# A router that works by halves of a row, behind the output projection of a two-layer decoder

## The chip, the cores and the metric

The kernel runs on one core of one Trainium2 chip. The metric is the device time of one execution in microseconds (us). Before the change the median of three runs is 1393.88 us (1393.7 to 1397.09).

## The reference

528 tokens (512 and 16 prepended meta tokens) of width 1024 pass two layers, float32 throughout. Layer 0 mixes tokens with a short gated convolution, layer 1 with attention over a shared latent. Behind each mixer stands a mixture of experts, and this is the part that matters here:

```
h = h + (mixer output) @ w_out              # 1024 x 1024
xf = rmsnorm(h, g)
g_logits = xf @ w_grp                       # 8 groups
e_logits = (xf @ w_exp).reshape(n, 8, 8)    # 8 experts in each group
grp   = argmax(g_logits)                    # one group per token
e_in  = e_logits[grp];  top 2 of 8 experts in it
gate  = max(softmax(g_logits)) * top_p / sum(top_p)
y     = sum over the two experts of gate * (silu(x @ w_gate) * (x @ w_up)) @ w_down
h = h + y
```

There are 64 experts in each layer with three matrices of 1024 x 256 floats, 1 MB each. All of them are read in each layer. At the end a last RMSNorm is taken and the 512 tokens are written.

## The kernel before

The residual stream `h` lies in SBUF as four tiles of 128 tokens and, in layer 0, a fifth tile of the 16 meta tokens (`META`). A tile is 128 tokens by 1024.

**Weights.** All large weights pass through one ring of 8 KB-per-partition slots (`Ring`, L67). They are loaded in the order of use by the queue of SyncE (SP, line L101). A load is issued when a slot comes free, and the router's weights are a load of their own (L347): in layer 0 on the same queue, in layer 1 on ScalarE's. GpSimdE multiplies them by the norm's gain (L348).

**Output projection** (`project_out`, L256). It is done for two halves of 512 output columns. In a half each tile has a PSUM bank (tag `acc`, five banks), and the contraction is walked in steps of one or two blocks of 128 rows; a block is three fp32r matmuls per tile (high and low parts of both operands, L292). Before a step its weight rows are split into high and low parts by ScalarE (L211) and VectorE (L212). The meta tile uses plain fp32 matmuls in four quarters of a bank (L274); ScalarE copies them into the scratch tile `x0[0]`, and a matmul with `fold` adds the quarters into a bank with the tag `misc` (L286). When the last step of a tile is done, VectorE adds the bank to `h` (L294). After the second half of a tile, `done(t)` calls the router for it.

**Router** (`Moe.route`, L363, one tile). ScalarE squares the row with a sum (L231), with `x0[0]` as its waste output, and GpSimdE makes the scale of the norm (L232, L233). TensorE transposes the row in two sets of four 128 x 128 blocks (L372) through one bank with the tag `tp`; the first set is copied out by ScalarE into `hT` (one buffer, L375), the second by VectorE into `x0[1]` (L377). Eight fp32 matmuls (each is two records in the trace) make 72 logits in the bank `misc` (L380), which has one buffer. VectorE then works out group and experts (L383 to L403), and two small copies are ScalarE's (L388, L396); the result is a mask `M`. `rank` (L409) counts, with small bf16 matmuls into a bank `rk`, which place each token has in its group (L417, L422, L425), and VectorE makes a selection matrix `d` (L418 to L421).

**First gather and experts.** `first_gather` (L457) collects the first group's tokens with matmuls of `d` and `h` (L431), scales them, and selects the tokens of the first four experts (L450). Then `run` starts: `gate_up` (L585, L589) multiplies with the gate and up weights of four experts and releases their slots, `down` (L628, L621) with the down weights. 16 such steps of four experts make a layer.

**Order.** Outside of `run`, where TensorE's order is that of the text, a planner orders the instructions of each engine: it simulates them with a cost model and takes, of what is ready, what stands first in the text. On the chip each engine then works off its list in order.

The function that is called for each finished tile is given here:

```
project_out(..., zH, zL, zM, STEPS[0], lambda t: moe0.route(t, psum))      # layer 0, L976
project_out(..., *oT[1], None, STEPS[1], lambda t: moe1.route(t, psum))    # layer 1, L1342
```

Of the kernel before, what the change touches and what calls it, by code (L numbers as in the profile page):

```python
# [9 lines left out]
F32 = mybir.dt.float32  # L10
F32R = mybir.dt.float32r
BF16 = mybir.dt.bfloat16
I32 = mybir.dt.int32
AF = mybir.ActivationFunctionType
ALU = mybir.AluOpType
# [4 lines left out]
P = 128  # L20
D = 1024
# [3 lines left out]
META = 4  # L25
NE = 64
CAP = 32
EPS = 1e-6
# [8 lines left out]
STEPS = ((0,), (1,), (2,), (3,), (4,), (5,), (6, 7)), ((4,), (5,), (6, 7))  # L37
# [79 lines left out]
def trunk_kernel(ctx: ExitStack, tc: tile.TileContext, x, meta, const, masks, rope, gcol, grow, wr, w_in, w_out, w_a, w_qr, w_hp,  # L117
# [17 lines left out]
    for l in range(2):  # L135
        for a in range(4):
            c = G_FFN + 8 * l + 2 * a
# [97 lines left out]
    def chunk(t, k):  # L235
        return h[t][:rows(t)].rearrange("r (a p b) -> r a b p", a=4, b=2)[:, k // 2, k % 2]
# [19 lines left out]
    def project_out(weights, psum, name, zH, zL, zM, steps, done):  # L256


        tiles = ((META,) if zM is not None else ()) + (0, 1, 2, 3)
        off = 0 if zM is not None else NM  # L260
        base = 0 if zM is not None else 4
        first, last = steps[0][0], steps[-1][-1]
        for half in range(2):
            ps = {t: psum.tile([P, 512], F32, tag="acc", name="acc", bufs=5) for t in tiles}
            for step in steps:
                w = {}
                for j in step:
                    kg, v = j // 4, j % 4
                    raw = ring.get((name, half, kg))[:, v]
                    w[j] = weights(j)  # L270
                    split(*w[j], raw)
                    if v == 3:
                        for i in range(4 if zM is not None else 0):
                            T.matmul(ps[META][32 * i:32 * i + 32], zM[:, j - 3 + i], ring.get((name, half, kg))[:, i],  # L274
                                     start=j - 3 == first, stop=j == last)
                        ring.release((name, half, kg))
                for t in tiles:
                    n = rows(t)
                    hh = h[t][:n, 512 * half:512 * half + 512]
                    pt = ps[t]  # L280
                    if t == META:
                        if last in step:
                            sm = moe0.x0[0].rearrange("p a s -> p (a s)")
                            A.activation(sm, pt, AF.Copy)
                            pt = psum.tile([P, 512], F32, tag="misc", name="misc", bufs=1)
                            T.matmul(pt[:n], fold, sm, start=True, stop=True)  # L286
                    else:
                        c = col0(t) - off
                        for j in step:
                            wH, wL = w[j]  # L290
                            for m, (l, r) in enumerate(((zH, wH), (zH, wL), (zL, wH))):
                                T.matmul(pt, l[:, j - base, c:c + n], r, start=j == first and m == 0, stop=j == last and m == 2)  # L292
                    if last in step:
                        V.tensor_tensor(hh, hh, pt[:n], op=ALU.add)  # L294
                        if half == 1:
                            done(t)


    class Moe:
# [35 lines left out]
        def prepare(self, limit):  # L335

            nT = self.nT
            n = NR[self.layer]
            m = n - TOP[self.layer]
            if self.layer == 1:  # L340
                self.first_tiles("right")
            R = self.R = [(pool(self.right if i < m else self.top, f"ringR{self.layer}{i}", side="right"), f"R{i}") for i in range(n)]
            for i in RIGHT[self.layer]:
                ring.open([R[i]], limit if i >= m else None)
            rp = self.rp = pool(self.temp, f"rt{self.layer}", 2, side="right")
            self.wg = rp.tile([P, 8, 72], F32, name="wg", bufs=1)
            (nc.scalar if self.layer else nc.sync).dma_start(self.wg, wr[self.layer].rearrange("p (a c) -> p a c", a=8))  # L347
            G.tensor_tensor(self.wg, self.wg, self.g[:, :, None].to_broadcast([P, 8, 72]), op=ALU.mult)  # L348
            self.rks = ExitStack()
            self.rkp = pool(self.rks, f"rk{self.layer}", side="right", space=PSUM)  # L350
            self.M = rp.tile([P, nT, 72], BF16, name="M", bufs=1)
            self.gl = rp.tile([P, nT, 8], F32, name="gl", bufs=1)
            self.gm = rp.tile([P, nT, 1], F32, name="gm", bufs=1)
            self.s8 = rp.tile([P, nT, 8], F32, name="s8", bufs=1)
            self.r8 = rp.tile([P, nT, 8], F32, name="r8", bufs=1)
            self.done = []
            G.tensor_copy(self.aux[:, :, 8], tok1[:, :nT])
            if nT == 5:
                for a in (self.gl, self.gm, self.oh, self.s8, self.r8, self.M):
                    G.memset(a[:, META], 0.0)  # L360
                G.memset(self.rstd[:, META:], 1.0)

        def route(self, t, psum):  # L363

            rp, n = self.rp, rows(t)
            rs = self.rstd[:n, t:t + 1]
            rstd_of(rp, rs, h[t][:n], n, D, junk=self.x0[0].rearrange("p k s -> p (k s)").bitcast(BF16))
            hT = []
            for u in range(2):
                ps = psum.tile([P, 4, P], F32, tag="tp", name="tp", bufs=1)  # L370
                for k in range(4):
                    T.transpose(ps[:, k, :n], chunk(t, 4 * u + k), ident[:n, :n])  # L372
                hT.append(rp.tile([P, 4, P], F32, tag="hT", name="hT", bufs=1) if u == 0 else self.x0[1])
                if u == 0:
                    A.activation(hT[u][:, :, :n], ps[:, :, :n], AF.Copy)  # L375
                else:
                    V.tensor_copy(hT[u][:, :, :n], ps[:, :, :n])  # L377
            ps = psum.tile([P, 512], F32, tag="misc", name="misc", bufs=1)
            for k in range(8):
                T.matmul(ps[:n, :72], hT[k // 4][:, k % 4, :n], self.wg[:, k], start=k == 0, stop=k == 7)  # L380

            gl, gm, oh = self.gl[:n, t], self.gm[:n, t], self.oh[:n, t]
            V.reduce_max(gm, ps[:n, :8], axis=AX)  # L383
            V.scalar_tensor_tensor(oh, ps[:n, :8], gm, rev8[:n], op0=ALU.is_equal, op1=ALU.mult)
            mg = rp.tile([P, 1], F32, tag="mg", name="mg")[:n]
            V.reduce_max(mg, oh, axis=AX)
            V.tensor_scalar(oh, oh, mg, None, op0=ALU.is_equal)
            A.activation(self.M[:n, t, NE:], oh, AF.Copy)  # L388

            se = rp.tile([P, 8, 8], F32, tag="se", name="se", bufs=1)[:n]  # L390
            gt = rp.tile([P, 8, 8], F32, tag="gt", name="gt", bufs=1)[:n]
            eq = rp.tile([P, 8, 8], F32, tag="eq", name="eq", bufs=1)[:n]
            s8, r8, M = self.s8[:n, t], self.r8[:n, t], self.M
            sh = [n, 8, 8]
            V.tensor_tensor(se, ps[:n, 8:72].rearrange("p (g e) -> p g e", g=8), oh[:, :, None].to_broadcast(sh), op=ALU.mult)
            A.activation(gl, ps[:n, :8], AF.Copy)  # L396
            V.reduce_sum(s8, se.rearrange("p g e -> p e g"), axis=AX)
            V.tensor_tensor(eq, s8[:, None, :].to_broadcast(sh), s8[:, :, None].to_broadcast(sh), op=ALU.is_equal)
            V.tensor_tensor(gt, s8[:, None, :].to_broadcast(sh), s8[:, :, None].to_broadcast(sh), op=ALU.is_gt)
            V.tensor_tensor(eq, eq, before8[:n], op=ALU.mult)  # L400
            V.tensor_tensor(gt, gt, eq, op=ALU.add)
            V.reduce_sum(r8, gt, axis=AX)
            V.scalar_tensor_tensor(M[:n, t, :NE].rearrange("p (g e) -> p g e", g=8), r8[:, None, :].to_broadcast(sh), 2.0,  # L403
                                   oh[:, :, None].to_broadcast(sh), op0=ALU.is_lt, op1=ALU.mult)
            self.done.append(t)
            if len(self.done) < self.nT:
                self.rank(t)
# [474 lines left out]
    with ExitStack() as l0:  # L882
# [10 lines left out]
        with ExitStack() as l0a:  # L893
# [44 lines left out]
            for j in range(4):  # L938
                W = []
                for s in range(3):  # L940
# [33 lines left out]
        wp = pool(l0, "wp0b", 2)  # L974
        psum = pool(l0, "ps0b", space=PSUM)
        project_out(lambda j: [wp.tile([P, 512], F32R, tag=a, name=a) for a in ("wH", "wL")], psum, "out", zH, zL, zM, STEPS[0],  # L976
                    lambda t: moe0.route(t, psum))
        moe0.first_gather(psum)


# [358 lines left out]
            whole[:] = weights(SLOT)  # L1339
        return [w[:, 512 * (j - 4):512 * (j - 3)] for w in whole]  # L1340

    project_out(part, psum, "o", *oT[1], None, STEPS[1], lambda t: moe1.route(t, psum))  # L1342
    moe1.first_gather(psum)
    psum_stack.close()
    oproj.close()
# [129 lines left out]
```

## Time and profile before

| | before |
|---|---|
| median of three runs | 1393.88 us |
| the profiled execution | 1390.24 us |
| its span, first to last instruction | 1388.4 us |
| TensorE busy (weight loads apart) | 1243.8 us, 90% |
| VectorE, ScalarE, GpSimdE busy | 507.5, 313.5, 53.6 us |
| HBM read and written | 434.40 and 2.10 MB, 314 GB/s over the span |
| TensorE clock granted, mean | 0.96 |

The table is of one execution, taken by the hardware profiler. Engines have short names in the views: PE is TensorE's matmuls and PEld its weight loads, DVE is VectorE, ACT ScalarE, POOL GpSimdE, SP SyncE; a q behind a name is that engine's issue of DMAs. L292 is line 292 of the kernel before. Times are us from the span's start. The ends of matmuls are modelled, so that a stretch in which PE is busy throughout is not by that alone one at its peak; the distance of the starts tells more. In a row of instructions, what stands in brackets is the idle time of the engine before it and what ended it.

### The profile page before, as it was taken

To read this page: it belongs to the slowest core of one execution; us is meant where nothing else is said; L and a number is where in the kernel's file an instruction comes from. 1 tells how busy PE (TensorE), PEld (TensorE's weight loads), DVE (VectorE), ACT (ScalarE), POOL (GpSimd) and SP (SyncE) were. 2 spreads that over 40 slices of the span, in tenths; PEclk is the share of its full clock that TensorE was granted. 3 is DMA by queue.
4 is the path that set the end of the run, shared out by engine and by line. 5 is a ranking of instruction groups with operands and counts; after the bars stand their busy time and mean duration, and the time that the engine had idled before them with its cause. 6 is when DMAs were issued, how large, how long until landed. Compare 5 with 4: busy or idle time off the path is not lost.

```text
span 1388.4 us, 22912 instructions
## 1 busy us (share of the span) xinstructions
PE 1243.8 (90%) x9647; PEld 794.1 (57%) x9647; DVE 507.5 (37%) x1220; ACT 313.5 (23%) x712; POOL 53.6 (4%) x146
## 2 busy tenths in 40 slices
PE   7999999999888888879799999999988788888885
PEld 7999866544444344434388888864543334433432
DVE  5555336132231312234246776462230212213024
ACT  6333123011010010121154765231110010101013
POOL 2100101000000000000021000010000000000001
PEclk9999999999999999989999999999999998999998
DMA  7422563899999999999910022949999999999994
GB/s 285 154 91 90 208 253 154 351 420 420 419 419 420 419 421 418 420 420 421 366 41 28 32 92 101 369 179 418 419 420 419 421 418 421 420 419 420 420 418 173
DMA packets 65954, 438.09 MB, mean 316 GB/s; under 512 B 7457, under 2 KB 7841, under 8 KB 15282
## 3 DMA queue, kind: packets, MB, share of 16 engines
q1 hardware_dynamic: 64432, 434.74, 76.8%
q10 hardware_dynamic: 1154, 1.78, 0.4%
q8 instruction: 78, 1.28, 0.4%
q14 instruction: 34, 0.28, 0.1%
q0 software_dynamic: 256, 0.01, 0.0%
HBM read 434.40 MB, written 2.10 MB: 314 GB/s over the span
## 4 chain that ended last, share of the span: by engine, by line
DMA 26%; PE 21%; ACT 1%; DVE 1%; issue 1%; POOL 0%; POOLq 0%; ACTq 0%; SPq 0%; DVEq 0%
DMA R<-in_w_gate_dram 6%; DMA B<-in_w_down_dram 4%; DMA B<-in_w_up_dram 4%; DMA R<-in_w_up_dram 3%; DMA A<-in_w_up_dram 3%; PE gu L589 2%; PE a L1062 2%; PE sc L1225 2%; PE pj L1319 2%; PE acc L292 2%; DMA A<-in_w_gate_dram 1%; DMA A<-in_w_down_dram 1%; DMA B<-in_w_gate_dram 1%; DMA R<-in_w_down_dram 1%; PE pj L1205 1%; PE ot L1274 1%
## 5 line engine op out<-in xcount | busy, mean ns | idle before, releaser
L589 PE MATMUL gu<-R,xT 128*32 128x256 f32 x1856 | 161.7, 409 | 34.3 <-DMA R<-in_w_up_dram 19.4
L589 PE MATMUL gu<-B,xT 128*32 128x256 f32 x1376 | 148.3, 438 | 38.7 <-DMA B<-in_w_gate_dram 22.1
L589 PEld LDWEIGHTS gu<-R,xT 128*32 128x32 f32 x1856 | 77.7, 117 | 107.6 <-issue 30.3
L589 PEld LDWEIGHTS gu<-B,xT 128*32 128x32 f32 x1376 | 66.9, 125 | 99.6 <-DMA B<-in_w_gate_dram 30.6
L589 PE MATMUL gu<-A,xT 128*32 128x256 f32 x720 | 101.3, 421 | 18.6 <-DMA A<-in_w_up_dram 11.8
L431 PE MATMUL w<-h,d 128*128 128x512 f32 x224 | 99.7, 598 | 0.0
L562 DVE COPY ag<-w 128x18 f32<-128x18 f32 x14 | 2.5, 177 | 240.0 <-PE w L561 240.0
L596 ACT ACTIVATE sg<-gu 128x256 f32<-128x256 f32 x32 | 12.3, 385 | 327.9 <-PE gu L589 327.9
L631 ACT ACTIVATE y<-dn 128x512 f32<-128x512 f32 x60 | 35.8, 597 | 198.1 <-PE dn L621 191.0
L950 PE MATMUL acc<-xH,wH 128*128 128x264 f32 x384 | 79.1, 286 | 0.0
L950 PE MATMUL acc<-xL,wH 128*128 128x264 f32 x384 | 78.8, 286 | 0.0
L950 PE MATMUL acc<-xH,wL 128*128 128x264 f32 x384 | 77.6, 283 | 0.0
L589 PEld LDWEIGHTS gu<-A,xT 128*32 128x32 f32 x720 | 45.8, 120 | 51.8 <-DMA A<-in_w_up_dram 15.7
L657 PE MATMUL w<-yHL,d 128*128 128x512 f32 (+1 forms) x252 | 73.0, 422 | 0.3
L659 DVE TENSOR_TENSOR h<-h,w 128x512 f32<-128x512 f32 x112 | 69.6, 679 | 0.8 <-PE w L657 0.5
L450 PE MATMUL w<-sel,xg 128*128 128x128 f32 x480 | 64.8, 292 | 4.5 <-ACT xg L436 4.5
L431 PEld LDWEIGHTS w<-h,d 128*128 128x128 f32 x224 | 41.4, 190 | 47.1 <-issue 46.4
L215 ACT ACTIVATE wH<-A,gc 128x256 fp32r<-128x256 f32 (+1 forms) x119 | 52.8, 520 | 59.0 <-PE acc L950 35.5
L450 PEld LDWEIGHTS w<-sel,xg 128*128 128x128 f32 x480 | 60.7, 205 | 7.2 <-ACT xg L436 7.2
L621 PE MATMUL dn<-R,sg 128*32 128x512 f32 x472 | 63.7, 595 | 0.0
L950 PEld LDWEIGHTS acc<-xL,wH 128*128 128x128 f32 x384 | 59.9, 188 | 0.2 <-DVE xL L212 0.2
L950 PEld LDWEIGHTS acc<-xH,wL 128*128 128x128 f32 x384 | 59.7, 189 | 0.0
(379 smaller groups left out, 2072.1 us busy)
## 6 DMA issues: line engine op xcount, KB each, us to landing
R<-in_w_up_dram SPq DMA_DIRECT2D x58, 1024.0 KB, 19.9
R<-in_w_down_dram SPq DMA_DIRECT2D x58, 1024.0 KB, 19.9
R<-in_w_gate_dram SPq DMA_DIRECT2D x58, 1024.0 KB, 19.9
B<-in_w_gate_dram SPq DMA_DIRECT2D x44, 1024.0 KB, 19.8
B<-in_w_up_dram SPq DMA_DIRECT2D x42, 1024.0 KB, 19.8
B<-in_w_down_dram SPq DMA_DIRECT2D x32, 1024.0 KB, 19.8
A<-in_w_down_dram SPq DMA_DIRECT2D x27, 1024.0 KB, 19.8
A<-in_w_gate_dram SPq DMA_DIRECT2D x26, 1024.0 KB, 19.9
```

Source lines behind the costliest of these rows:

```text
L215: i = A.activation(H, src, AF.Copy, scale=g)
L292: T.matmul(pt, l[:, j - base, c:c + n], r, start=j == first and m == 0, stop=j == last and m == 2)
L431: i = T.matmul(ps[u], d, h[t][:n, 512 * u:512 * u + 512], start=first, stop=last, skip_group_check=True)
L450: T.matmul(ps[:, k], self.xg[:, 4 * u + k], self.sel[q], start=True, stop=True)
L589: T.matmul(gu[CAP * e:CAP * e + CAP, s], xT[k // 4][:, k % 4, CAP * e:CAP * e + CAP], w[e][:, k], start=k == 0, stop=k == 7)
L621: T.matmul(dn[CAP * e:CAP * e + CAP, :n], hT[:, b, CAP * e:CAP * e + CAP], w[:, b, c:c + n], start=b == 0, stop=b == 1)
L631: A.activation(y[:, u], down_part(q, hT, u, 0, 512 * u, 512), AF.Copy)
L657: T.matmul(ps[:m, :n], DT[t], a, start=i == 0, stop=i == 1)
L659: V.tensor_tensor(hh, hh, ps[:m, :n], op=ALU.add)
L950: T.matmul(ps[:, u, :HALF], l[:, k, P * m:P * m + P], r[:, k, HALF * u:HALF * u + HALF], start=k == 0 and l is wH and r is xH, stop=k == 7 ...
L1062: T.matmul(a[:n, b, :c1 - c0], l[:, k, :n], r[:, k, c0:c1], start=k == 0 and m == 0, stop=k == 7 and m == 2)
L1225: T.matmul(ps[u][:, :w], l[:, q], r[:, w * u:w * u + w], start=m == 0, stop=m == 4 and u < nb - 1)
```

## The change

The router gets a second argument, the half `u`, and is called after both halves of a tile. At the first call it takes the squares of the first 512 columns, the first four transposes and the first four logit matmuls; at the second the rest, and then everything as before. The sums of squares lie in a new small tile `sq`, and GpSimdE adds the halves up. The logits of all tiles lie side by side in one bank, which is held from the first call on (`lg`, 72 columns per tile); only the very first matmul in it has the start flag. Tile 0 comes ahead of the meta tile in both halves, and the meta tile's fold uses the transposes' bank.

```diff
     def project_out(weights, psum, name, zH, zL, zM, steps, done):
-        tiles = ((META,) if zM is not None else ()) + (0, 1, 2, 3)
+        tiles = (0,) + ((META,) if zM is not None else ()) + (1, 2, 3)
...
                             A.activation(sm, pt, AF.Copy)
-                            pt = psum.tile([P, 512], F32, tag="misc", name="misc", bufs=1)
+                            pt = psum.tile([P, 512], F32, tag="tp", name="fold", bufs=1)
                             T.matmul(pt[:n], fold, sm, start=True, stop=True)
...
                     if last in step:
                         V.tensor_tensor(hh, hh, pt[:n], op=ALU.add)
-                        if half == 1:
-                            done(t)
+                        done(t, half)
...
             self.r8 = rp.tile([P, nT, 8], F32, name="r8", bufs=1)
+            self.sq = rp.tile([P, nT, 2], F32, name="sq", bufs=1)
+            self.lg = None
...
-        def route(self, t, psum):
+        def route(self, t, u, psum):
 
             rp, n = self.rp, rows(t)
-            rs = self.rstd[:n, t:t + 1]
-            rstd_of(rp, rs, h[t][:n], n, D, junk=self.x0[0].rearrange("p k s -> p (k s)").bitcast(BF16))
-            hT = []
-            for u in range(2):
-                ps = psum.tile([P, 4, P], F32, tag="tp", name="tp", bufs=1)
-                for k in range(4):
-                    T.transpose(ps[:, k, :n], chunk(t, 4 * u + k), ident[:n, :n])
-                hT.append(rp.tile([P, 4, P], F32, tag="hT", name="hT", bufs=1) if u == 0 else self.x0[1])
-                if u == 0:
-                    A.activation(hT[u][:, :, :n], ps[:, :, :n], AF.Copy)
-                else:
-                    V.tensor_copy(hT[u][:, :, :n], ps[:, :, :n])
-            ps = psum.tile([P, 512], F32, tag="misc", name="misc", bufs=1)
-            for k in range(8):
-                T.matmul(ps[:n, :72], hT[k // 4][:, k % 4, :n], self.wg[:, k], start=k == 0, stop=k == 7)
+            rs, c = self.rstd[:n, t:t + 1], slice(512 * u, 512 * u + 512)
+            junk = self.x0[0].rearrange("p k s -> p (k s)").bitcast(BF16)
+            A.activation(junk[:n, :512], h[t][:n, c], AF.Square, accum_out=self.sq[:n, t, u:u + 1])
+            G.tensor_scalar(self.sq[:n, t, u:u + 1], self.sq[:n, t, u:u + 1], 1.0 / D, EPS if u == 0 else self.sq[:n, t, 0:1],
+                            op0=ALU.mult, op1=ALU.add)
+            ps = psum.tile([P, 4, P], F32, tag="tp", name="tp", bufs=1)
+            for k in range(4):
+                T.transpose(ps[:, k, :n], chunk(t, 4 * u + k), ident[:n, :n])
+            if u == 0:
+                hT = rp.tile([P, 4, P], F32, tag="hT", name="hT", bufs=1)
+                A.activation(hT[:, :, :n], ps[:, :, :n], AF.Copy)
+            else:
+                hT = self.x0[1]
+                V.tensor_copy(hT[:, :, :n], ps[:, :, :n])
+            if self.lg is None:
+                self.lg = psum.tile([P, 512], F32, tag="misc", name="misc", bufs=1)
+                assert n == P
+            ps = self.lg[:, 72 * t:72 * t + 72]
+            for k in range(4):
+                T.matmul(ps[:n], hT[:, k, :n], self.wg[:, 4 * u + k], start=u == 0 and t == 0 and k == 0, stop=u == 1 and k == 3,
+                         skip_group_check=True)
+            if u == 0:
+                return
+            G.tensor_tensor(rs, self.sq[:n, t, 1:2], nhalf[:n], op=ALU.pow)
...
-                    lambda t: moe0.route(t, psum))
+                    lambda t, u: moe0.route(t, u, psum))
...
-    project_out(part, psum, "o", *oT[1], None, STEPS[1], lambda t: moe1.route(t, psum))
+    project_out(part, psum, "o", *oT[1], None, STEPS[1], lambda t, u: moe1.route(t, u, psum))
```

## Rows read from the trace of the kernel before

**Rows 1.** The page's 40 slices of the span: busy share of DMA in tenths.

```profile
DMA  7422563899999999999910022949999999999994
```

**Rows 2.** Windows over both expert stages: length, engines' busy us (instructions), PEclk, DMA share, GB/s.

```profile
244.00:640.00 396.00, 352.84 (x2960) 176.28 (x2952) 102.54 (x216) 49.02 (x98) 0.00 (x0) 0.95 1.00 415
...
937.00:1385.00 448.00, 375.91 (x3151) 185.71 (x3139) 110.55 (x225) 55.79 (x113) 5.05 (x12) 0.94 0.98 404
```

**Rows 3.** Load queue in time (start, length, engine, line, what), first loads after each silence.

```profile
247.04 0.80 SPq L101 DMA_DIRECT2D R<-in_w_down_dram  x2
...
935.52 0.81 SPq L101 DMA_DIRECT2D A<-in_w_down_dram  x2
```

**Rows 4.** Windows: PE, PEld, DVE, ACT, POOL busy; layer 0's second half and tail, layer 1's.

```profile
186.00:204.00 18.00, 18.00 (x86) 12.86 (x84) 4.26 (x7) 3.90 (x7) 1.15 (x1) 1.00 0.37 146
...
204.00:223.00 19.00, 19.00 (x118) 13.66 (x118) 11.77 (x48) 8.90 (x21) 4.62 (x15) 1.00 0.40 141
223.00:230.00 7.00, 7.00 (x32) 5.78 (x32) 2.52 (x10) 0.00 (x0) 0.00 (x0) 0.52 1.01 425
230.00:244.00 14.00, 12.77 (x75) 7.89 (x77) 10.68 (x55) 4.14 (x10) 0.00 (x0) 1.00 0.12 49
884.70:902.50 17.80, 17.80 (x80) 14.75 (x80) 6.52 (x10) 2.68 (x5) 1.15 (x1) 1.00 0.96 385
902.50:924.60 22.10, 22.05 (x145) 17.60 (x144) 15.79 (x63) 7.87 (x20) 3.73 (x12) 1.00 0.68 264
924.60:931.85 7.25, 4.65 (x24) 2.88 (x25) 5.57 (x33) 2.98 (x5) 0.00 (x0) 1.00 0.08 33
```

**Rows 5.** Timeline of PE in layer 1: transposes and logits between projection matmuls.

```profile
902.56 0.63 PE L372 MATMUL tp<-cs,h 128*128 128x128 f32 x4
902.94 0.47 PE L292 MATMUL acc<-wH,oH 128*128 128x512 f32 x1
903.26 0.40 PE L292 MATMUL acc<-wL,oH 128*128 128x512 f32 x1
...
904.46 1.01 PE L380 MATMUL misc<-wg,hT 128*128 128x72 f32 x8
905.27 0.48 PE L292 MATMUL acc<-wL,oH 128*128 128x512 f32 x1
```

**Rows 6.** Timeline of DVE in layer 1: first add; last tile's chain and rank.

```profile
902.75 0.69 DVE L294 TENSOR_TENSOR h<-h,acc 128x512 f32<-128x512 f32 x1 [6.12 <-PE acc L292]
...
922.38 0.16 DVE L383 TENSOR_REDUCE gm<-misc 128x1 f32<-128x8 f32 x1
...
924.90 0.22 DVE L403 SCALAR_TENSOR_TENSOR M<-r,oh 128x64 bf16<-128x64 f32 x1
925.42 0.23 DVE L418 SCALAR_TENSOR_TENSOR rm<-rk,M 128x72 f32<-128x72 f32 x1 [0.30 <-PE rk L417]
...
925.89 0.26 DVE L421 TENSOR_REDUCE aux<-rm 128x8 f32<-128x64 f32 x1
```

**Rows 7.** Layer 0's router weights and first-half add; the masks' landing time and conversion.

```profile
186.68 1.15 POOL L348 TENSOR_TENSOR wg<-wg,gc 128x576 f32<-128x576 f32 x1 [27.62 <-DMA wg<-in_wr_dram]
...
180.28 0.69 DVE L294 TENSOR_TENSOR h<-h,acc 128x512 f32<-128x512 f32 x1
...
8.03 0.33 SPq L890 DMA_DIRECT2D xT<-in_masks_dram  x1
...
DMA to landing us min/median/max: 12.2/12.2/12.2
...
24.68 0.29 POOL L891 CAST tri_b<-xT 128x128 bf16<-128x128 f32 x1
```

**Rows 8.** Timeline of PE: the meta tile's gather, first gate/up matmuls of both layers.

```profile
221.63 1.12 PE L431 MATMUL acc<-hm,d 16*128 16x512 f32 x2
...
243.37 7.11 PE L589 MATMUL gu<-R,xT 128*32 128x256 f32 x128
...
931.85 0.41 PE L589 MATMUL gu<-A,xT 128*32 128x256 f32 x2 [0.78 <-DVE xT L451]
```

## The prediction

> **What bounds the kernel now.** I read the page's row of DMA load in 40 slices first, then busy time by stretch, then the load queue, then the engines in order of time around both routers. The DMA row [rows 1] stands at 9 in slices 8 to 19 and 27 to 38, counted from 0: both expert stages run at the rate of their weights, 415 and 404 GB/s, while TensorE idles there (352.8 of 396 us in the first) [rows 2]. So an expert stage lasts as long as its loads, and these are held up by one thing: with all slots full the queue is silent until the first gate/up matmuls of that layer release a slot. In layer 0 the DMA share is 0.12 in 230 to 244 [rows 4] and the next load goes out at 247.0; in layer 1 the next goes out at 935.5 [rows 3]. Whatever moves the first gate/up matmul (243.4 and 931.9 [rows 8]) therefore moves the end of the kernel one for one, once per layer. The change works just ahead of these two points.
>
> What bounds that stretch? In the second half of the output projection TensorE is busy 18.00 of 18.00 us (layer 0, 186 to 204) and 17.80 of 17.80 (layer 1, both halves), 80 matmuls at 0.223 us each [rows 4]. And in the router's tail too: 19.00 of 19.00 and 7.00 of 7.00 in layer 0, 22.05 of 22.10 in layer 1. Only at the very end does it idle, 7.25 - 4.65 = 2.6 us in layer 1 and 14.00 - 12.77 = 1.2 in layer 0. Latency chains are there, but gathers and the remaining projection matmuls fill them. In layer 0 one thing more is lost: in 223 to 230 the granted clock is 0.52 [rows 4], mostly at 1.2 GHz. That stretch costs 7.0 x (1 - 0.52) = 3.4 us.
>
> **The change part by part.** *Work moved.* For each tile four transposes and four chunks of logits (eight matmul records) leave the tail and go into the second half's matmuls. Four transposes take 902.94 - 902.56 = 0.38 us and the projection matmul behind them 903.26 - 902.94 = 0.32 instead of 0.22, so 0.10 more; the logits 905.27 - 904.46 = 0.81 [rows 5] and again 0.10. That is 1.39 us per tile, 5.6 us in layer 1, all of it added to a stretch without a gap; in layer 0 the 16-row tile is bounded by 0 and 1.39, I take 0.7, so 6.3 us. The tail loses the same work, 0.38 + 0.81 = 1.19 per tile, and between none and all of the switches, since there they partly stood beside other fp32 work. So TensorE's sum over both stretches does not fall: it rises by 0 to 0.8 us per layer, I take 0.4.
>
> *Layer 1.* TensorE's floor is before, plus 0.4, less the idle that could be filled: of the 2.6 us, all but about 1.0 is the closing chain (gathered tokens, selection, first xT), which is not touched. So -0.6 at best. The other end is VectorE, whose work in the tail stays whole: add 0.69 and a copy of the same 512 columns, the chain from group maximum to mask 922.38 to 925.13 = 2.75, rank 925.42 to 926.15 = 0.73 [rows 6]: 4.86 us per tile, 19.4 for four if nothing overlaps. Before, the tail from the first add (902.75 [rows 6]) to the last rank took 926.15 - 902.75 = 23.4. After, it starts 5.6 later. With 19.4 and about 2 of lead-in for the first tile (transposes, copy, logits) it ends 21.4 - (23.4 - 5.6) = 3.6 later than before. VectorE was in fact busy 15.79 us in 902.5 to 924.6 [rows 4], nearer to 17 for the whole tail than to 19.4, so the lower end is the nearer: +1.2.
>
> The waits in the tail change little. The logits of a tile now go into the shared bank, and must still wait until VectorE and ScalarE have read the previous tile's; with the one-buffered bank of before they did that too. The 16-row tile's fold takes the transposes' bank, which delays the next transposes by its 1.0 us matmul and an add; the tail has over 4 us per tile, so that is covered. The scratch copy for the fold now follows tile 0's square on ScalarE, about 1.5 us, covered by projection matmuls of the other tiles (0 to 0.5 uncovered, I take 0).
>
> *Layer 0.* If the low-clock stretch goes, -3.4 + 0.4 + 0.5 (VectorE, as above but with one more tile as cover) = -2.5. If it stays, +0.4 + 0.5 = +0.9. The 16-row gathers just ahead of it (two records of 1.1 us, at 221.6 [rows 8]) are in the changed kernel as well. I take the middle, -0.8.
>
> *ScalarE, GpSimdE.* Two half squares for one whole one, one more small GpSimdE operation per tile. ScalarE is busy 3.90 of 18 us in the second half, VectorE 4.26 [rows 4], but the splits of the next weight rows run on both, in order, and now can stand behind a square or a copy of about 0.6 us. A row of weights lasts 12 matmuls, 2.7 us, its two splits are 512-column operations of about 0.7 each [rows 6], so some 1 us is in hand: 0 to 1 us in all, I take 0.5. GpSimdE's results are first needed by the gathers, 20 us later: nothing.
>
> *Loads.* The last early loads are released by the last projection matmuls. In layer 0 they have landed by about 232 (share 0.12 from 230 on [rows 4]), 11 us ahead of the first gate/up; a few us later costs nothing, and from 11 us on it costs one for one.
>
> *A new wait.* In layer 0 the first half's logits need the router weights. GpSimdE scales these as soon as they land, at 186.7 to 187.8, after a wait of 27.6 us; tile 0's first-half add is at 180.3 [rows 7], and with tile 0 ahead of the 16-row tile about 179.5. Transposes and copy bring its logits to about 181.5. If they stand there in TensorE's queue, everything behind them, the whole second half, waits: 0 to 6.3 us. If the planner put them behind enough matmuls, nothing. What it thinks of such a load: the masks, issued at 8.0 behind the first weights, landed 12.2 us later, at 20.2, and the planner put their conversion at 24.7, behind operations that were written later but that it took to be ready sooner [rows 7]. It was pessimistic there, so I take 0.
>
> Sum: 1.2 - 0.8 + 0.5 = +0.9, so 1390.24 + 0.9 = 1391.1 us for an execution like the profiled one (span 1388.4 and 1.8 around it). The median of the runs shown is 1393.88, 3.6 above it: 1394.8.
>
> The Trainium skill's page "TensorE: Matmul & The Clock Gate", section "Part 4: PE-mode transpose", says that transposes do not count towards the full clock as matmuls do. Against it stands that layer 1 has as many transposes per tile and stays at 1.00, and that the clock fell after a stretch with TensorE busy all the time [rows 4]. By the rule the drop would go, since half of the transposes leave the tail: the second rival below.
>
> **Rivals.** *One: the tail is latency after all.* Ends of matmuls are modelled, so "busy" may cover waits; then the tail loses its 6.3 and 5.6 us, and the second halves take the work in without growing: -11.9 + 0.9 = -11 us, 1383. For: VectorE's chain is serial per tile. Against: 0.223 us per projection matmul leaves no room, and the tail's pieces start without gaps. 0.12.
>
> *Two: the low-clock stretch goes and the tail packs well.* -2.5 in layer 0, -0.6 in layer 1, 0.5 for the splits: -2.6, 1391.3; at best, with no cost of switches, VectorE or splits, -3.4 - 1.0 = -4.4, 1389.5. For: fewer small operations stand ahead of it. Against: the 16-row gathers stay. 0.12.
>
> *Three, slower: the router weights stop TensorE in layer 0.* It decides from the point where tile 0's first-half logits reach the head of the queue before 187.8; each us earlier costs one. Worst 6.3 + 0.9 = +7.2, 1401.1; from half of it on, +4.1, 1398.0, it can be told. Against: the masks. 0.17.
>
> *Four: the planner leaves the first halves in the tail,* since it orders by readiness and not by the text: 0, 1393.9. In the order of before it did take ready transposes ahead of projection matmuls. 0.05.
>
> **How the numbers follow.** Forecast 0.54; its own range, from the bounds (layer 1 -0.6 to +3.6, layer 0 -2.5 to +0.9, splits 0 to 1: -3.1 to +5.5), is 1391 to 1399. A measurement tells about 0.3%, 4.2 us, from no change. Faster: rival one, 0.05 of rival two at its best, 0.03 of the forecast: 0.20. Slower: rival three 0.17 and 0.07 of the forecast, where VectorE's end holds in both layers: 0.24. Same: the rest, 0.56. The range leaves rival one out and reaches to the end of rival three: 1389 to 1401.
>
> **What would show it.** Right: transposes and logits of all tiles between the projection's second-half matmuls, these as dense as before; that half longer by 5 to 7 us per layer; the tail shorter by about as much; more idle TensorE in the tail; first gate/up within 3 us of before in each layer. Wrong: the first gate/up over 4 us earlier (rivals one and two, told apart by the granted clock around 230), or TensorE waiting on the router weights around 182 to 188 (three). An expert stage that does not shift with its first gate/up would break the one-for-one rule.

## The result and the profile after

The changed kernel takes 1402.17 us (median of six runs, 1400.04 to 1404.54) against 1393.10 for the kernel before (six runs, 1390.76 to 1397.09): a ratio of 1.0057, with an interval of 1.0042 to 1.0072. It is slower by about 8 us, 7.4 us above the 1394.8 that was predicted and 1.2 us above the range, which ended at 1401. The profiled execution has a span of 1398.2 us, 9.8 above the 1388.4 of before.

Where do the 9.8 us arise? The next fence has windows of the kernel after (length; PE, PEld, DVE, ACT, POOL busy; granted clock; DMA share; GB/s). The first runs from the first projection matmul of layer 0 to its first gate/up matmul, the last is the same for layer 1.

```profile
157.81:252.44 94.63, 91.00 (x416) 59.87 (x415) 38.77 (x134) 24.57 (x57) 8.51 (x27) 0.91 0.54 215
186.60:204.00 17.40, 17.40 (x96) 12.69 (x95) 3.59 (x6) 5.34 (x13) 2.25 (x4) 1.00 0.39 145
204.00:223.00 19.00, 19.00 (x101) 13.37 (x100) 8.05 (x24) 6.12 (x15) 3.54 (x11) 1.00 0.21 63
232.00:252.44 20.44, 18.52 (x53) 9.39 (x53) 10.72 (x61) 3.76 (x9) 0.00 (x0) 0.58 0.18 76
894.10:943.66 49.56, 45.89 (x249) 34.75 (x248) 26.71 (x105) 15.27 (x38) 6.07 (x17) 1.00 0.65 261
```

The same two windows of the kernel before:

```profile
157.43:243.37 85.94, 84.07 (x417) 59.14 (x415) 39.64 (x134) 23.23 (x47) 6.67 (x22) 0.96 0.59 236
884.74:931.85 47.11, 44.47 (x248) 35.19 (x248) 27.83 (x105) 13.53 (x30) 4.88 (x13) 1.00 0.69 274
```

Layer 0's stretch grew by 94.63 - 85.94 = 8.69 us, layer 1's by 49.56 - 47.11 = 2.45. The rest is small: the stretch starts 0.38 later; from layer 0's first gate/up to layer 1's projection it is 641.66 us against 641.37; and behind layer 1's first gate/up 2.01 us come back (454.54 against 456.55). The sum is 0.38 + 8.69 + 0.29 + 2.45 - 2.01 = 9.8. Most of what comes back is the last gate/up step, whose matmuls ran at the lower clock before and not after. That is not the work of the change: e12 below, whose layer 1 is that of before, has the short piece too (3.64 us), e5 the long one (5.33). The last such piece in the chain of waits, before and then after:

```profile
1355.81 5.33 PE gu L589 x58
```

```profile
1367.53 3.64 PE gu L599 x58
```

The lines that answer to [rows 8], [rows 7] and [rows 5], from the timeline of the kernel after (start, length, engine, line, operation):

```profile
180.25 0.75 PE L374 MATMUL tp<-cs,h 128*128 128x128 f32 x4
180.75 0.47 PE L292 MATMUL acc<-wL,zH 128*128 128x512 f32 x1
181.06 0.39 PE L292 MATMUL acc<-wH,zL 128*128 128x512 f32 x1
...
189.01 1.15 POOL L347 TENSOR_TENSOR wg<-wg,gc 128x576 f32<-128x576 f32 x1
...
195.82 0.90 PE L386 MATMUL misc<-wg,hT 128*128 128x72 f32 x7
...
229.67 1.10 PE L441 MATMUL acc<-hm,d 16*128 16x512 f32 x2
230.70 1.11 PE L386 MATMUL misc<-wg,xT 128*128 128x72 f32 x8
231.74 1.59 PE L441 MATMUL acc<-hm,d 16*128 16x512 f32 x2
...
234.16 2.07 PE L441 MATMUL acc<-h,d 128*128 128x512 f32 x2
...
252.44 3.88 PE L599 MATMUL gu<-R,xT 128*32 128x256 f32 x68
```

The change does what it says: transposes and logits stand among the second half's matmuls, four transposes taking 0.50 us (180.25 to 180.75) and the matmul behind them 0.31, where the prediction had 0.38 and 0.32. Half 2 stays dense (17.40 of 17.40 us), and VectorE, which in 204 to 223 was busy 11.77 us before [rows 4], is so for 8.05: its chains start later. The router weights are scaled at 189.0, and TensorE first uses them at 195.8, without a wait. What is new comes late. The meta tile's gathers are at 229.7 and 231.7 instead of 220.5 and 221.6, and behind them the next gather takes 2.07 us: from 232 to the first gate/up the granted clock is 0.58, most of it spent at 1.2 GHz. Before, the low stretch took some 7 us at 0.52 [rows 4].

The second new thing is idle TensorE in the tail. Who it waited for, in layer 0 from 205 us to the first gate/up: after, then before (the wait; total us, times, longest).

```profile
PE rk L432 <- DVE rm L428: 1.0, 3, 0.3
PE acc L460 <- ACT xg L446: 0.8, 1, 0.8
PE tp L374 <- DVE xT L380: 0.5, 1, 0.5
PE tp L374 <- DVE rm L428: 0.3, 1, 0.3
PE acc L477 <- DVE oh L397: 0.3, 1, 0.3
```

```profile
PE acc L450 <- ACT xg L436: 0.8, 1, 0.8
PE rk L422 <- DVE rm L418: 0.3, 1, 0.3
```

### The profile page after: what moved, and what is told of

Same layout as the page of the kernel before. It is cut to its first block, busy times and chain, and to the rows that moved or that the text cites. A ratio compares the mean times of both kernels' runs of the same rounds, so it can differ in the third digit from the quotient of the medians.

```text
span 1398.2 us, 22957 instructions
## 1 busy us (share of the span) xinstructions
PE 1250.7 (89%) x9647; PEld 793.6 (57%) x9647; DVE 505.3 (36%) x1220; ACT 316.3 (23%) x730; POOL 56.6 (4%) x155
## 3 DMA queue, kind: packets, MB, share of 16 engines
q8 instruction: 78, 1.28, 0.4%
## 5 line engine op out<-in xcount | busy, mean ns | idle before, releaser
L599 PE MATMUL gu<-R,xT 128*32 128x256 f32 x1856 | 158.9, 399 | 36.6 <-DMA R<-in_w_up_dram 25.6
L599 PE MATMUL gu<-B,xT 128*32 128x256 f32 x1376 | 145.5, 437 | 36.3 <-DMA B<-in_w_gate_dram 18.4
```

The costliest lines, as they stand in the source:

```text
L599: T.matmul(gu[CAP * e:CAP * e + CAP, s], xT[k // 4][:, k % 4, CAP * e:CAP * e + CAP], w[e][:, k], start=k == 0, stop=k == 7)
```

## The experiments

Every experiment is read by the same two windows as above, from the first projection matmul to the first gate/up matmul of the layer, in the one traced execution of each kernel. These are steadier than the whole: layer 1's window is 47.11 to 47.14 us in all seven kernels whose layer 1 is that of before. The stretch between the two windows is not: it takes 641.4 to 648.3 us over the fourteen traces, with the same code in it, and the traces of before and after happen to have the two shortest. The whole kernel's time varies by several us between executions of one kernel, so each time stands beside that of the kernel before from the same chip: 1394.08 us for e1 to e4, 1395.71 for e5 to e8, 1393.65 for e9 to e12.

**e1 and e2: the change in one layer alone.** The other layer keeps the whole route of before.

```
 e1:  project_out(..., lambda t, u: moe1.route_whole(t, psum) if u else None)
 e2:  project_out(..., lambda t, u: moe0.route_whole(t, psum) if u else None)   # and the meta tile first
```

> Halves in layer 0 alone; layer 1 routes whole rows as before. Theory A (the loss is layer 0's longer stretch at 1.2 GHz, plus some switching): first gate/up of layer 0 again about 9 us later than before, low clock for about 16 us; layer 1 as before from there; total +7 to +9 us, about 1401. Theory B (VectorE's chain bounds both tails, the clock is a side issue): each layer carries its share, so about +4 to +5 here, 1397.5.

> Halves in layer 1 alone; layer 0 as before. Theory A: +2.5 us at layer 1's first gate/up, as between the two traces (1.0 of it TensorE idle, 1.4 TensorE work), total about +2 to +3, 1395.5; no low clock in layer 1's tail. Theory B: +4 to +5, 1397.5.

Measured: e1 1400.89 us (1391.62 to 1403.02 over nine runs, two of them near 1392), ratio 1.0025 (1.0004 to 1.0046); e2 1395.32 (1390.87 to 1399.51), ratio 1.0002 (0.9988 to 1.0017). Windows of e1, then of e2:

```profile
158.01:252.60 94.59, 90.97 (x417) 59.89 (x415) 38.75 (x134) 24.56 (x57) 8.49 (x27) 0.91 0.54 215
897.59:944.73 47.14, 44.49 (x248) 35.23 (x248) 27.81 (x105) 13.51 (x30) 4.86 (x13) 1.00 0.69 274
```

```profile
158.41:244.21 85.80, 83.92 (x416) 58.60 (x414) 39.60 (x134) 23.23 (x47) 6.65 (x22) 0.96 0.60 237
890.13:939.71 49.58, 45.92 (x249) 34.78 (x248) 26.71 (x105) 15.27 (x38) 6.04 (x17) 1.00 0.66 261
```

The layers do not touch each other: e1 has layer 0's window of after (94.59) and layer 1's of before (47.14), e2 the reverse. Layer 0 carries the loss. The two runs of e1 near 1392 show a higher mean clock (0.960 and 0.962) than the other seven (0.952 to 0.959), so the long low stretch may have stayed away in them; no trace of them is kept. In the whole time layer 1's 2.5 us can't be told from nothing.

**e3 and e4: the meta gathers over 128 rows,** in the kernel after and the kernel before.

```
+    G.memset(h[META], 0.0)
     nc.sync.dma_start(h[META][:NM], meta)
 ...
-            n, d = rows(t), self.d[:rows(t), t].bitcast(F32)
+            d = self.d[:, t].bitcast(F32)
-                i = T.matmul(ps[u], d, h[t][:n, 512 * u:512 * u + 512], ...)
+                i = T.matmul(ps[u], d, h[t][:, 512 * u:512 * u + 512], ...)
```

> The changed kernel, with the meta tile's gather matmuls over 128 rows in place of 16 (rows 16 to 127 are zero on both sides); same number of matmuls and columns. Theory A1 (the 16-row gathers set off the low clock): no low-clock stretch in layer 0's tail, 8 us saved, first gate/up about 244, total about 1394. Theory A2 (it is the thinner tail as a whole, small matmuls and waits): the low stretch stays, total about 1402.

> The kernel before with the meta tile's gather matmuls over 128 rows in place of 16. Theory A1: its low-clock stretch of 6.6 us goes, first gate/up 3.3 us earlier, total about 1390, so that this kernel beats both. Theory A2: unchanged, 1393.

Measured: e3 1399.22 us (1396.75 to 1401.9), ratio 1.0033 (1.0021 to 1.0046); e4 1394.3 (1391.58 to 1395.65), ratio 1.000 (0.9988 to 1.0012). Windows of e3, then of e4:

```profile
159.66:246.81 87.15, 83.30 (x416) 56.78 (x414) 38.67 (x134) 24.58 (x57) 8.49 (x27) 1.00 0.58 233
894.01:943.57 49.56, 45.90 (x248) 34.73 (x247) 26.71 (x105) 15.27 (x38) 6.11 (x17) 1.00 0.65 261
```

```profile
161.41:243.91 82.50, 80.63 (x417) 56.78 (x415) 39.52 (x134) 23.23 (x47) 6.65 (x22) 1.00 0.62 246
```

With 128 rows the clock stays at 1.00 in both. The low stretch had therefore cost 85.94 - 82.50 = 3.4 us before and 94.63 - 87.15 = 7.5 after: 4.0 of the 8.7 us. The other 4.65 us (87.15 against 82.50) are no matter of the clock. That e4 is no faster as a whole has its reason, in the trace, ahead of the window: the projection starts 4.0 us later than before. The memset comes before the first load; that it is what delays the start is argued, not shown (e3, with the same memset, starts 1.9 us later than the kernel after).

**e5: the same padding without the memset,** the free rows filled late from the input (the selection matrix is zero there).

```
+        nc.scalar.dma_start(h[META][NM:128], x[:128 - NM])
         project_out(lambda j: ...)
```

> The kernel before, with rows 16 to 127 of the meta tile's buffer filled by one late transfer from the input, so that the meta gathers run over 128 rows with no memset ahead of the first load. Theory A (the 16-row gathers bring the low clock, and in e4 the memset's 4 us at the start ate the gain): the projection starts at 157.4 to 158 as before, the granted clock stays at 1.00 through the layer-0 tail, that stretch takes 82.5 us as in e4 instead of 85.9, and the kernel takes 3.4 us less than the kernel before: about 1390.7 against 1394.1. Rival (the clock followed from what the memset changed at the start, not from the rows): the clock falls again near 223 to 230 and the time is that of before.

Measured: 1392.28 us (1389.18 to 1393.37), ratio 0.997 (0.9957 to 0.9982). Windows of e5:

```profile
159.22:241.74 82.52, 80.64 (x417) 56.77 (x415) 39.55 (x134) 23.23 (x47) 6.65 (x22) 1.00 0.61 246
887.78:934.92 47.14, 44.48 (x248) 35.21 (x248) 27.84 (x105) 13.52 (x30) 5.20 (x13) 1.00 0.68 274
```

As theory A has it: 82.52 us at full clock, and now a gain of 3.4 us in the medians, though the projection starts 1.8 us later here, not at 157.4 to 158.

**e6: the code of the change without its early start.**

```
-                    lambda t, u: moe0.route(t, u, psum))
+                    lambda t, u: [moe0.route(t, v, psum) for v in range(2)] if u else None)
```

(the same in layer 1, and the fill of e5)

> The kernel after, with the same fill, and with both halves of a tile's router, transposes and logits issued only when the second half of its row is complete: the code of the change (one bank, two square sums, power on GpSimd, tile 0 first), none of its early start. Theory B (the halves done early push every projection of half 2 later and so all five route chains, and VectorE's chain then stands open in the tail): the stretch from the projection's start to the first gate/up falls from 87.2 (e3) to about 83, idle TensorE in it from 3.9 to about 2, and the same in layer 1 from 49.6 to about 47.3; the kernel takes about 1391 to 1393. Rival C (the cost is in the form: more switches, the one bank, tile 0 ahead of the meta tile): the stretch stays near 87 and the kernel near 1397.

Measured: 1394.62 us (1391.32 to 1395.61), ratio 0.9986 (0.9977 to 0.9996). Windows of e6:

```profile
159.09:243.00 83.91, 81.34 (x416) 56.71 (x414) 40.41 (x134) 24.04 (x57) 8.23 (x27) 1.00 0.61 242
889.33:936.90 47.57, 44.86 (x249) 34.98 (x248) 27.72 (x105) 14.73 (x38) 6.05 (x17) 1.00 0.67 272
```

Theory B has the stretch nearly right (83.91 for about 83); the kernel's time is 1.6 us above its 1391 to 1393. Rival C falls. Starting early costs 87.15 - 83.91 = 3.24 us in layer 0 and 49.56 - 47.57 = 1.99 in layer 1; the form (all else that the change brings: one bank, two sums of squares, tile 0 first) costs 83.91 - 82.52 = 1.39 and 0.43. Idle TensorE goes from 1.88 (e5) over 2.57 (e6) to 3.85 (e3), its busy time from 80.64 over 81.34 to 83.30. So of the early start's 3.24 us 1.28 are idle and 1.96 are busy time; of layer 1's 1.99 us it is 0.95 and 1.04.

**e7 and e8: the place of the meta tile,** gathers over 16 rows again. e7 is the kernel after with the meta tile first in half 2; e8 is the kernel before with tile 0 first.

```
 e7:
-                for t in tiles:
+                for t in tiles if half == 0 or zM is None else (META, 0, 1, 2, 3):
 e8:
-        tiles = ((META,) if zM is not None else ()) + (0, 1, 2, 3)
+        tiles = (0,) + ((META,) if zM is not None else ()) + (1, 2, 3)
```

> The kernel after with the meta tile again ahead of tile 0 in half 2 of layer 0 (half 1 keeps tile 0 first), its gathers over 16 rows. Theory D (the low clock lasts as long as the sparse rest of the tail lets it; the change put the meta gathers second and so 8 us later, into the rank chain): the meta gathers come first again, the low stretch shrinks from 16 towards 7 us, the first gate/up of layer 0 comes at 247 to 249 instead of 252.4, and the kernel takes 1397 to 1399. Rival E (the length does not hang on the place of the gathers): the low stretch keeps 14 to 17 us, and the time stays within 1.5 us of the kernel after, 1400 to 1403.

> The kernel before with only the order of the tiles changed, tile 0 ahead of the meta tile in both halves of layer 0's output projection; routes whole as before, gathers over 16 rows. Theory D: the meta gathers move from about 221 to 224 or later, where TensorE is still dense behind them, so the low stretch stays between 6 and 10 us and the time rises by 0 to 2 us: 1394 to 1396. Rival F (the order alone makes the loss): the low stretch grows to 14 us or more and the time rises by 4 us or more, to 1398 or above.

Measured: e7 1401.9 us (1398.15 to 1402.84), ratio 1.0036 (1.0023 to 1.005); e8 1391.78 (1387.67 to 1392.86), ratio 0.9967 (0.9956 to 0.9978). Windows and gathers of e7, then of e8:

```profile
157.84:248.45 90.61, 87.81 (x416) 59.16 (x415) 38.60 (x134) 24.88 (x57) 8.45 (x27) 0.94 0.56 224
225.50:236.00 10.50, 10.50 (x35) 6.54 (x35) 4.44 (x21) 0.39 (x2) 0.92 (x3) 0.51 1.02 428
```

```profile
224.41 1.10 PE L441 MATMUL acc<-hm,d 16*128 16x512 f32 x2
225.44 1.89 PE L386 MATMUL misc<-wg,xT 128*128 128x72 f32 x8
227.26 2.07 PE L441 MATMUL acc<-hm,d 16*128 16x512 f32 x2
```

```profile
157.83:240.69 82.86, 80.34 (x416) 56.82 (x415) 40.27 (x134) 23.12 (x47) 6.67 (x22) 1.00 0.62 245
```

```profile
222.18 1.10 PE L431 MATMUL acc<-hm,d 16*128 16x512 f32 x2
223.21 0.75 PE L372 MATMUL tp<-cs,h 128*128 128x128 f32 x4
223.80 1.01 PE L380 MATMUL misc<-wg,hT 128*128 128x72 f32 x8
...
224.98 1.10 PE L431 MATMUL acc<-hm,d 16*128 16x512 f32 x2
```

In e7 the window is 4.0 us shorter than in the kernel after (90.61 against 94.63) and the low stretch takes some 10 us, as theory D has it (248.45 for the first gate/up, expected 247 to 249). Its time is above the 1397 to 1399 expected and within rival E's 1400 to 1403; by the ratio it is 0.2% below the kernel after (1.0036 against 1.0057, with intervals that just overlap). In e8 both D and F missed, on the good side: the clock does not fall at all, although the gathers have 16 rows, and a change of one line makes the kernel faster by 0.33%. Its two gathers are 2.8 us apart with transposes and logits over 128 rows between them; before, one followed the other with only a rank matmul between (220.46 and 221.63). So few rows are what the low clock needs in these kernels, but not enough by themselves. Work over 128 rows between the gathers does not tell the cases apart either: in e7 the gathers are 2.85 us apart (224.41 and 227.26) with logits over 128 rows between them, and the clock fell right behind the first, as those logits show (1.89 us, 1.01 in e8); in the kernel after logits stand between them too (the gathers start at 229.67 and 231.74). What in the surroundings counts is open.

**e9 and e10: which tiles start early** (form of e6, with the fill). e9 gives the early start to tiles 2 and 3, e10 to tile 0 and the meta tile (the start flag goes with whichever logits come first).

```
 e9:   [moe0.route(t, v, psum) for v in ((u,) if t in (2, 3) else range(2) if u else ())]
 e10:  ... if t in (0, META) ...       (in layer 1 tile 0)
```

> The kernel of e6 with the early start given back to tiles 2 and 3 alone, in both layers (the other tiles issue both halves at the end of their row); filled meta rows. Theory G (the transposes and logits of the later tiles are what TensorE does while a rank step of an earlier tile waits for VectorE; moved ahead, they leave those waits open): nearly the whole cost of the early start comes with these two tiles. From the projection's start to the first gate/up: layer 0 85.5 to 87 us (e6 83.9, all tiles early 87.2), layer 1 48.9 to 49.6 (e6 47.6, all early 49.6). Rival H (every early half costs alike, by the switches between projection and small matmuls): layer 0 85.2, layer 1 48.6 or less, with the rank waits no longer than in e6.

> The counterpart of e9: only the tiles that come first, tile 0 and the meta tile (in layer 1 tile 0), start early. Theory G: the later tiles' transposes and logits stay between the rank steps, so little is lost: layer 0 83.9 to 84.7 us, layer 1 47.4 to 47.9. Rival H: layer 0 85.2, layer 1 48.1.

Measured: e9 1397.21 us (1393.46 to 1401.1), ratio 1.0024 (1.0013 to 1.0035); e10 1397.53 (1394.2 to 1399.07), ratio 1.0018 (1.0005 to 1.0032). Windows of e9, then of e10:

```profile
158.89:244.79 85.90, 82.63 (x417) 57.21 (x415) 39.69 (x134) 24.45 (x57) 7.98 (x27) 1.00 0.59 236
889.11:938.34 49.23, 45.68 (x249) 35.03 (x248) 26.82 (x105) 14.90 (x38) 6.23 (x17) 1.00 0.65 263
```

```profile
158.26:244.21 85.95, 82.71 (x416) 56.74 (x415) 40.81 (x134) 24.50 (x57) 8.27 (x27) 1.00 0.60 236
891.77:939.68 47.91, 45.20 (x248) 34.85 (x247) 27.69 (x105) 14.85 (x38) 5.99 (x17) 1.00 0.67 270
```

In layer 1 theory G holds: tiles 2 and 3 cost 49.23 - 47.57 = 1.66 of the 1.99 us, tile 0 costs 0.34, all of it busy time. TensorE's waits for masks and rank steps from 905 us to the first gate/up, in e6 and then in e9 (total us, times, longest), grow from 1.0 to 1.7 us:

```profile
PE rk L427 <- DVE M L413: 0.7, 1, 0.7
PE rk L432 <- DVE rm L428: 0.3, 1, 0.3
```

```profile
PE rk L433 <- DVE rm L429: 1.7, 3, 1.0
```

In layer 0 theory G does not hold: e9 lies in its range, e10 1.2 us above. Each pair costs 2.0 us, 1.3 to 1.4 of them busy time and 0.7 idle, alike, as rival H has it, but more than its 1.3, and together more than all five tiles (3.24). There the early start costs in more than one way, and the shares don't add. Each edit also makes the planner lay out the engines' order anew, which no run here holds fixed. Why TensorE's busy time rises is not settled; ends of matmuls are modelled, and part of it may be waits.

**e11 and e12: both cures together, and half of one.** e11 is e8 with the fill, e12 is e5 with 32 rows.

```
 e12:  n = 32 if t == META else P
       d = self.d[:n, t].bitcast(F32)
       nc.scalar.dma_start(h[META][NM:32], x[:32 - NM])
```

> The kernel before with both of the edits that took the low clock away, tile 0 ahead of the meta tile (e8) and filled meta rows (e5). If both did it by the clock alone they do not add: layer 0's stretch takes 82.3 to 83 us as in each of them and the kernel 1390 to 1392, 3 to 4.5 us below the kernel before. If the order gave a gain of its own beside the clock, the stretch takes under 81.5 us and the kernel about 1388.

> The kernel before with the meta gathers over 32 rows instead of 16 (rows 16 to 31 filled, as in e5, where it was 128). If the number of rows that a matmul works on counts in proportion, 32 of 128 is still little and the clock falls again near 223 to 230: layer 0's stretch 85 to 86 us, the time that of before. If any doubling is enough, the clock stays at 1.00, the stretch takes 82.5 us, the time is about 3.4 us less.

Measured: e11 1391.88 us (1388.64 to 1393.92), ratio 0.9982 (0.9971 to 0.9993); e12 1392.96 (1388.12 to 1397.84), ratio 0.9995 (0.9981 to 1.0009). Windows of e11, then of e12:

```profile
159.18:241.92 82.74, 80.23 (x416) 57.10 (x414) 40.17 (x134) 23.11 (x47) 6.63 (x22) 1.00 0.62 245
```

```profile
158.09:243.94 85.85, 83.98 (x417) 59.15 (x415) 39.61 (x134) 23.24 (x47) 6.66 (x22) 0.96 0.59 236
225.00:230.00 5.00, 5.00 (x21) 3.78 (x21) 0.91 (x5) 0.00 (x0) 0.00 (x0) 0.50 1.01 428
```

The two cures do not add: each takes away the same low stretch (82.74 us together; 82.52 and 82.86 alone). The whole time gained 1.8 us against the kernel before, less than the 3 to 4.5 expected, in part because the projection starts 1.75 us later with the fill. With 32 rows the clock falls as with 16 (85.85 us, 0.50 in 225 to 230), so one doubling is not enough. e8, a change of one line, and e5 are the fastest, 0.33% and 0.30% below the kernel before; these two can't be told apart.

## Why the prediction was wrong, point by point

| layer 0's window | us | against the line above |
|---|---|---|
| before | 85.94 | |
| without the low clock (e5) | 82.52 | -3.42 |
| + form of the change (e6) | 83.91 | +1.39 |
| + early start (e3) | 87.15 | +3.24 |
| + low clock of the kernel after | 94.63 | +7.48 |

**The step that failed** is layer 0: "If the low-clock stretch goes ... = -2.5. If it stays, +0.4 + 0.5 = +0.9 ... I take the middle, -0.8." It neither went nor stayed: it grew from 3.4 us lost to 7.5. The text weighed the gathers' presence ("in the changed kernel as well") and never asked what would stand around them. The order of tiles alone took the fall away (e8); with the early start too, it came and lasted longer. That dense work had then gone ahead of the gathers, into half 2, is a likely reason, not a shown one. That the fall hangs on the 16-row gathers is shown (e3, e4, e5: gone with 128 rows), and that its length depends on the order of the tiles is what one trace each shows (e7: 90.61 against 94.63). Just how the surroundings set off and lengthen it stays open.

**Two terms were too small.** "It rises by 0 to 0.8 us per layer, I take 0.4": busy time rose by 1.42 in layer 1 (44.47 to 45.89), and in layer 0, at full clock, by 2.66 (80.64 to 83.30). And "VectorE, as above but with one more tile as cover", +0.5: idle rose by 1.97 (1.88 to 3.85). Layer 1 was forecast at +1.2 within -0.6 to +3.6 and came to +2.45: the mechanism as told (VectorE's chain starts later, TensorE idles more in the tail), the size double. The idle has a name now: the transposes and logits of later tiles had covered TensorE's waits for VectorE, and moving them ahead uncovers these. In layer 1 they are the rank steps (e9); in layer 0 the rank steps' part grows from 0.3 to 1.0 us, and waits for a copy, a mask step and one more rank step come to it (0.5, 0.3 and 0.3 above). The prediction's cover argument spoke of gathers and projection matmuls and left these out.

The term behind both is "The tail loses the same work, 0.38 + 0.81 = 1.19 per tile". The last projection matmul of layer 0, in e5 and in e3 (both at full clock):

```profile
219.19 0.39 PE L292 MATMUL acc<-wH,zL 128*128 128x512 f32 x1
```

```profile
224.41 0.48 PE L293 MATMUL acc<-wH,zL 128*128 128x512 f32 x1
```

Up to it, the stretch grew from 59.97 to 64.75 us; behind it, up to the first gate/up, it went from 22.55 to 22.40. So 4.8 us were paid in front and 0.15 came back. In layer 1 it is 3.4 us in front and 1.0 back.

**What was right.** The one-for-one rule, in the traced pair: from gate/up to the next projection 641.7 us, before 641.4, and the load queue's silence ends with it, at 256.1 in layer 0. That the two agree so closely is luck: this stretch varies by up to 6.9 us between the traces, and a whole time shows a shift of a few us only through the median of several runs. TensorE bounds half 2, so the work moved there is paid in full; rival one (-11 us) is out. Rival three's stall did not come: the scaling of the router weights was even later (189.0), behind five small square sums, but the planner had put the logits at 195.8; the +7.2 it would have given is near the measured loss, for another reason. Rival four is out, the halves were moved. Rival two had the sign of the clock wrong. The splits' +0.5 can't be told apart.

On the clock the Trainium skill's rule (page "TensorE: Matmul & The Clock Gate", section "Part 4: PE-mode transpose", that transposes do not count towards the full clock) did not decide here by itself: e5 has all of the transposes of before in its tail and stays at 1.00, and with half of them taken out of the tail the low stretch grew.

## What to carry to other kernels

Work that seems to lie on the path may be the cover for somebody's latency: before moving it ahead into a stretch that is dense already, ask what stands between a matmul and the vector step that it waits for once the work is gone; here the stretch was bound by TensorE, and the move gained nothing and opened these waits. Where a profile shows a low granted clock, find the instructions ahead of it and ask what the change puts around them, not only whether they stay. And change one thing at a time: the order of two tiles, put in as a side matter, was worth 0.33% in the kernel before (e8), and with the early start the same order went with a longer low stretch (94.63 us, 90.61 without it in half 2), so that the parts do not add.

## What the hardware showed that was not expected

In the kernel before TensorE was busy without a gap in 204 to 223 (19.00 of 19.00 us [rows 4]), and the clock fell right behind it; in 225 to 230 it stood at 0.50 with TensorE busy 5.00 of 5.00 us, in e12 and before:

```profile
225.00:230.00 5.00, 5.00 (x22) 3.78 (x22) 1.25 (x6) 0.00 (x0) 0.00 (x0) 0.50 1.01 426
```

So a TensorE that the trace shows as busy did not keep the clock up. In layer 0's tail the fall came behind the meta tile's gathers where these ran over 16 or 32 rows, and did not come where they ran over 128 (seven kernels: e3 to e6 and e9 to e11). It came with 16 rows in five kernels (before, after, e1, e2, e7), with 32 in one (e12), and not in e8, with 16. One execution of each was traced. What sets e8 apart is open: matmuls over 128 rows stood between its two gathers, but between those of the kernel after and of e7 as well.
